# Entry order, pool data, ring keys and last rows in a one-core macaron decoder block

## The chip, the cores and the metric

The kernel runs on one core of one Trainium2 chip. Five engines work side by side: TensorE (PE, matrix products, with its weight loads as PEld), VectorE (DVE), ScalarE (ACT), GpSimd (POOL) and SyncE (SP, which here only issues transfers). Each engine takes its own instructions strictly in order and waits on semaphores for the others. The metric is the time of one execution on the device in microseconds.

## The reference

Input x is 1024 tokens by 1024 channels in float32. With `rms` a normalisation of each token's row:

```python
h = x + 0.5 * swiglu(rms(x), w1a, w3a, w2a)        # swiglu = (silu(x@w1) * (x@w3)) @ w2, width 2816
u = rms(h)
q, k, v, p, gate_logits = split(u @ W_in)
yA = dilated_mixture_attention(q, k, v) @ W_A      # 3 groups of 4 heads: (window, dilation) (128,1) (512,4) (2048,16)
yB = multiscale_pool(p) @ W_B                      # 4 groups of 128 channels, trailing means over 2, 4, 8, 16
h = h + (sigmoid(gA) * yA + sigmoid(gB) * yB) @ W_o
h = h + 0.5 * swiglu(rms(h), w1b, w3b, w2b)
out = rms(h)
```

## The kernel before, in words

**The products.** Every float32 operand is split in a high part in fp32r (a copy by ACT) and a lower part (the rest, a subtraction by DVE or POOL). A product is then three matmuls: high by high, lower by high, high by lower. The large products go by a seven-product scheme on 2 x 2 blocks. The left operand X (tokens) exists as seven sums: b11, b21, b22 (blocks), t1, t2, t3, t4 (sums of blocks). Class `Quad` holds the four blocks of one right operand (weights); `operand(m)` makes the m-th sum of weights (for m6 two sums on DVE, L345 and L347, for m7 one, L351) and splits it (`split`: ACT L303, then POOL or DVE L306); `run(m)` puts 12 matmuls of 128x512 on PE (L314). m1 uses b11, m2 b21, m3 b22, m4 t4, m5 t1, m6 t2, m7 t3, in the order 1, 6, 2, 7, 5, 4, 3.

**The entries.** At three places the X sums of a new left operand must first be made: at the start of the first FFN (f1, from the start to about 70 us), at the combined input projection (mix, from about 667) and at the second FFN (f2, from about 1297). There `Entry.run` interleaves the making of the sums with products m1 and m2, which need only b11 and b21. Token tiles 4 to 7 come one after the other. For tile t: the row is scaled by its norm (`scaled_rows`, DVE L267, with the difference for t3 by POOL L430), transposed on PE (L381 and L455), copied by ACT (L382 in `Rows`, L398 in `Parts`) and its lower parts are made by DVE (L385 in `Rows`, L401 in `Parts`); the sums t1 (L460), t2 (`second`, L441) and t4 (`fourth`, L445) are made by DVE in between. Each tile takes two products, i before its transposes and k behind them, two operands for products to come, and `out(i)` and `out(k)`, which carry results out of PSUM (DVE or ACT). `more(0)` is the operand for product m6, the first one behind the entry, and `more(1)` the one after. All of this is an order written out by hand under a manual schedule, so the order of the calls is the order in each engine's queue.

**The pairs.** In `up` a `Pair` joins two quads (gate and up projection of the FFN). When it is done, `Pair.parts` makes the sums of its result for the second product (L582, L587, L588, L592) and spills each to DRAM through SP (L577).

**From mix to attention.** The input projection's products are spread over 'items'. At fixed places before the end loads for the attention stage are put on SP: the four pool blocks of 1 MiB (`load_pool`, L1234), which lie in places of X sums no longer needed (groups 2 and 3 in b11, groups 0 and 1 in b21), the values (`load_values`, L1227) and the weights and gates of the first branch product (`load_branch`, L1238 and L1239). `late_w` (L1184) and the gates (L1061) are stored through SP in the same stretch. Then attention runs: scores `s` (L1545), transposes `tp` (L1592), `o` (L1625), and the branch product `yp` (L1679), which takes its left operand from the pool blocks and its right from `wab`. The keys and queries of a head group are loaded by `load_ring` (L1197, L1198) into a ring of eight places.

**The output projection.** `step_o(i)` multiplies by part i of W_o (L1918). Its operand is split by `hi_o` (ACT L1901) and `lo_o` (DVE L1905). The last steps stand between the transposes for f2 (`rows_first2`, whose `lower` and `keep` are L385 and L389).

**The last product.** `Down` multiplies by w2 in steps (L753), splits its operands (L711, L715), sums weights where needed (L731) and adds into the rows (L758). At the last but one product, `low_half` squares the lower half of a row (ACT L2083), adds the epsilon (DVE L2084) and multiplies the half by the final gain (DVE L2085); at the last one `high_half` (L2090), `power` (L2094, L2095) and `send_out` (L2100 to L2104) finish the row.

Of the kernel before, what the change touches and what calls it, by code (L numbers as in the profile page):

```python
# [10 lines left out]
F32 = mybir.dt.float32  # L11
# [115 lines left out]
def tile_block(  # L127
# [275 lines left out]
    class Entry:  # L403
# [18 lines left out]
        def run(self, high, after, first=0):  # L422
# [11 lines left out]
            for t in range(4, NT):  # L434
# [16 lines left out]
                s = Rows(X, "b22", y[:, HIGHS], t)  # L451
# [4 lines left out]
                r3 = Rows(X, "t3", t3, t)  # L456
                t2 = bank("acc", f"x_t2_{t}")
                if last:
                    r2 = second()
                ve.tensor_tensor(p12, p12, b11, op=OP.subtract)  # L460
                r1 = Parts(X, "t1", p12, t)
                if not last:
                    s.lower()
                self.operand(i + 2)
                self.out(i)
                self.product(k)
                if last:
                    r2.lower()
                    r3.lower()
                    r1.lower()  # L470
                    self.more(1)
                    r4 = fourth()
                    s.lower()
                    r4.lower()
                else:
                    y, t3 = scaled_rows(t + 1)
                    r2 = second()
                    r1.lower()
                    r3.lower()
                    r2.lower()  # L480
                    r4 = fourth()
                    self.operand(k + 2)
                    r4.lower()
                self.out(k)
                after(t)
                if t == NT - 2:
# [3 lines left out]
    class Pair:  # L490
# [80 lines left out]
        def parts(self, place=None):  # L571
# [15 lines left out]
            ve.tensor_tensor(a21, a21, a11, op=OP.subtract)  # L587
            ve.tensor_tensor(a12, a12, a22, op=OP.subtract)  # L588
            spill(6, a12)
            spill(5, a21)  # L590
            e = both[:, lows] if place else self.sv.half_tile("u", f"{j}5")
            ve.tensor_tensor(e, a11, a22, op=OP.add)  # L592
            spill(0, e)

    def up(sv, sums, between, name, room, begun):
# [3 lines left out]
        with tc.manual_schedule():  # L599
# [6 lines left out]
            for k, (q, w, m, out) in enumerate(items):  # L606
# [4 lines left out]
                if k > 0:  # L611
# [4 lines left out]
                    if p is not q:  # L616
                        parts.append(p.parts())
# [224 lines left out]
    def begin_up1():  # L842
# [95 lines left out]
        def after(t):  # L938
            if t + 2 < NT:
                squares(t + 2, square2)  # L940
            if t == 5:
                raws.depth = 8
# [394 lines left out]
    X_mix.update(sums_of_x(mstack.enter_context(sbuf("xb")), "mix", ("b22", "t2", "t3", "t1", "t4")))  # L1337
# [14 lines left out]
    with tc.manual_schedule():  # L1352
# [4 lines left out]
        for k in range(len(items) + 4):  # L1357
# [29 lines left out]
            if k == len(items) - 5:  # L1387
                load_pool(2, "b11", 0)
                load_pool(3, "b11", 1)
            if k == len(items) - 4:  # L1390
                load_values(0, row_part)
                load_branch(0)
            if k == len(items) - 3:
# [822 lines left out]
```

## Time and profile before

| | us |
|---|---|
| three runs | 1952.91, 1947.35, 1949.93; median 1949.93 |
| the profiled execution | 1953.68 |
| its span | 1951.9 |
| PE busy in the span | 1909.9 (98%) |
| DVE, ACT, POOL busy | 1338.1, 777.0, 727.5 |
| moved by DMA | 333.56 MB, 171 GB/s in the mean |

A line of the profile such as `u_mixm<-xhi_t_mix,wc_mixm` names the tile written and the tiles read; f1, mix and f2 are told apart by the names' endings (`u_f1..`, `u_mixm`, `u_f2..`). Times in a timeline are from the span's start. The span counts from the first to the last recorded instruction, so it is a little shorter than the execution's own time.

### The profile page before, as it was taken

The page shows a single profiled execution, that of the slowest core. Times are in us where ns is not written, and L with a number is a line of the kernel's source. Part 1 is how long each engine was busy: PE and PEld are TensorE (multiplying, and loading weights), DVE is VectorE, ACT ScalarE, POOL GpSimd, SP SyncE. Part 2 cuts the span into 40 slices and gives each one's busy share as a digit, 9 for nine tenths or more (in the row PEclk, how much of TensorE's full clock was granted, in tenths as well). Part 3 has the DMA queues.
Part 4 walks back from the last instruction along what each step waited for, and adds up shares of the span by engine and source line. Part 5 has one row for each costly group of instructions (what it writes and reads, how often), then busy time and mean ns, then how long its engine had stood idle before and what let it go on. Part 6 is the DMA issues. An engine that isn't in the chain of part 4 may idle for free. (4 is left out here: it accounts for less than half of the span.)

```text
span 1951.9 us, 24861 instructions
## 1 busy us (share of the span) xinstructions
PE 1909.9 (98%) x8842; PEld 1571.3 (80%) x8842; DVE 1338.1 (69%) x2020; ACT 777.0 (40%) x1396; POOL 727.5 (37%) x555
## 2 busy tenths in 40 slices
PE   9999999999999999999998999999999999999998
PEld 7788888888888877888877888877788888878886
DVE  6777556658676776657874797777666556577777
ACT  6323332333345542334444673263333333333344
POOL 4333333332222344544544265643333333322132
PEclk9999999999999999999999999999999999999999
DMA  4154322336475526764568997642523323454564
GB/s 185 33 197 150 111 87 103 134 114 207 150 240 201 193 81 226 235 228 181 210 249 290 258 248 264 246 172 73 208 92 125 108 86 103 137 195 148 189 215 162
DMA packets 147437, 333.56 MB, mean 171 GB/s; under 512 B 20209, under 2 KB 40945, under 8 KB 145777
## 3 DMA queue, kind: packets, MB, share of 16 engines
q1 hardware_dynamic: 138096, 307.22, 46.8%
q10 hardware_dynamic: 9216, 24.75, 3.6%
q8 instruction: 70, 1.15, 0.2%
q14 instruction: 55, 0.44, 0.1%
HBM read 229.61 MB, written 102.30 MB: 170 GB/s over the span
## 5 line engine op out<-in xcount | busy, mean ns | idle before, releaser
L753 PE MATMUL d_f<-bhi_f,ahi_f 128*128 128x512 f32 x616 | 240.7, 391 | 1.7 <-ACT ahi_f L711 1.2
L753 PE MATMUL d_f<-bhi_f,alo_f 128*128 128x512 f32 x616 | 240.5, 390 | 1.7 <-POOL alo_f L715 1.3
L753 PE MATMUL d_f<-blo_f,ahi_f 128*128 128x512 f32 x616 | 239.7, 389 | 0.0
L715 POOL TENSOR_TENSOR alo_f<-g_f,ahi_f 128x512 fp32r<-128x512 f32 x68 | 96.7, 1439 | 282.9 <-ACT ahi_f L711 282.9
L314 PE MATMUL u_mixm<-xhi_t_mix,wc_mixm 128*128 128x512 f32 x608 | 197.3, 395 | 4.3 <-DVE xlo_t_mix L385 3.2
L314 PE MATMUL u_mixm<-xhi_b_mix,wc_mixm 128*128 128x512 f32 x456 | 149.2, 394 | 3.3 <-DVE y_m L1036 2.0
L314 PEld LDWEIGHTS u_mixm<-xhi_t_mix,wc_mixm 128*128 128x128 f32 x608 | 115.1, 190 | 30.2 <-ACT y_m L1030 3.6
L753 PEld LDWEIGHTS d_f<-bhi_f,alo_f 128*128 128x128 f32 x616 | 115.6, 188 | 28.0 <-POOL alo_f L715 2.6
L753 PEld LDWEIGHTS d_f<-bhi_f,ahi_f 128*128 128x128 f32 x616 | 115.6, 188 | 26.1 <-ACT ahi_f L711 1.6
L753 PEld LDWEIGHTS d_f<-blo_f,ahi_f 128*128 128x128 f32 x616 | 115.7, 188 | 23.8
L314 PE MATMUL u_mixm<-xlo_t_mix,wc_mixm 128*128 128x512 f32 x304 | 119.4, 393 | 0.0
L306 POOL TENSOR_TENSOR wc_mixm<-s_mixm,wc_mixm 128x512 fp32r<-128x512 f32 x52 | 74.2, 1428 | 103.7 <-ACT wc_mixm L303 88.3
L314 PEld LDWEIGHTS u_mixm<-xhi_b_mix,wc_mixm 128*128 128x128 f32 x456 | 85.1, 188 | 24.8 <-POOL wc_mixm L306 3.8
L303 ACT ACTIVATE wc_mixm<-s_mixm 128x512 fp32r<-128x512 f32 x76 | 47.8, 630 | 131.0 <-DVE s_mixm L347 56.7
L314 PE MATMUL u_mixm<-xlo_b_mix,wc_mixm 128*128 128x512 f32 x228 | 88.9, 390 | 0.0
L711 ACT ACTIVATE ahi_f<-g_f 128x1024 fp32r<-128x1024 f32 x84 | 81.8, 974 | 2.6 <-DMA g_f<-gs_f 2.5
L306 POOL TENSOR_TENSOR wc_mixm<-raw,wc_mixm 128x512 fp32r<-128x512 f32 x40 | 57.7, 1444 | 64.8 <-ACT wc_mixm L303 59.2
L1918 PE MATMUL wo<-w_o,o_hi 128*128 128x512 f32 x224 | 69.4, 391 | 0.3 <-ACT o_hi L1901 0.3
L711 ACT ACTIVATE bhi_f<-s_f2w 128x512 fp32r<-128x512 f32 x55 | 32.7, 627 | 91.5 <-DVE s_f2w L731 82.3
L314 PEld LDWEIGHTS u_mixm<-xlo_t_mix,wc_mixm 128*128 128x128 f32 x304 | 57.8, 190 | 12.0
L711 ACT ACTIVATE bhi_f<-s_f1w 128x512 fp32r<-128x512 f32 x55 | 33.1, 630 | 78.5 <-DVE s_f1w L731 73.5
L715 DVE TENSOR_TENSOR alo_f<-g_f,ahi_f 128x1024 fp32r<-128x1024 f32 (+1 forms) x44 | 52.7, 1197 | 7.1 <-ACT ahi_f L711 7.1
(1318 smaller groups left out, 5099.6 us busy)
## 6 DMA issues: line engine op xcount, KB each, us to landing
g_f<-gs_f SPq DMA_DIRECT2D x70, 512.0 KB, 4.5
gs_f<-y_f SPq DMA_DIRECT2D x88, 256.0 KB, 2.2
raw<-in_w2a_dram SPq DMA_DIRECT2D x35, 512.0 KB, 3.9
raw<-in_w2b_dram SPq DMA_DIRECT2D x35, 512.0 KB, 3.9
gs_f<-gb_f SPq DMA_DIRECT2D x46, 256.0 KB, 2.3
raw<-in_w1a_dram SPq DMA_DIRECT2D x22, 512.0 KB, 4.6
raw<-in_w3a_dram SPq DMA_DIRECT2D x22, 512.0 KB, 6.2
raw<-in_w1b_dram SPq DMA_DIRECT2D x22, 512.0 KB, 4.3
```

Of the source, the lines that this page charges most:

```text
L303: ac.activation(w[:, 0], src, AF.Copy)
L306: eng.tensor_tensor(w[:, 1], src, w[:, 0].bitcast(F32), op=OP.subtract)
L314: pe.matmul(p, a, b, start=(start and k == 0 and q == 0), stop=(k == 3 and q == 2), skip_group_check=not start)
L711: ac.activation(hi[:, c], src, AF.Copy)
L715: eng.tensor_tensor(lo[:, d], src[:, o], hi[:, d].bitcast(F32), op=OP.subtract)
L753: pe.matmul(self.banks[m][t], l, r, start=(first and q == 0), stop=(last and q == 2))
L1918: pe.matmul(banks[m][t], l, r, start=(st == 0 and j == 0 and q == 0), stop=(st == 1 and j == 1 and q == 2))
```

## The change

- In `Entry.run`, tiles 4 to 6: the operand for a later product follows its product at once; the lower part of the first sum (t1) comes ahead of the next tile's scaling; `out(k)` comes ahead of the fourth sum. In the last tile the transposes come in the order t3, p12, b22 instead of b22, p12, t3. `more(0)` moves from the end of tile 6 to the end of tile 5. As a count of splits decides which engine makes a lower part, the lower part of f2's m6 is made by POOL instead of DVE.
- In f1 the raw weights are loaded a piece deeper from each tile on.
- In `up`, the three sums of `Pair.parts` are made one per product, in another order, instead of all three behind one product.
- t2 of the mix lies in a pool of its own that lives on into attention. Pool groups 2 and 3 are loaded one product sooner, groups 0 and 1 two products sooner and into t2. The first branch's weights and gates are loaded ahead of the values. The keys of every second use go into quarters of b21's place, and the ring has four places instead of eight.
- In the output projection, the last operand is split behind the first two tiles' lower parts.
- In the last product, the four rows' products with the final gain stand together at the last tile of the last but one product, and the epsilon is added in `power`.

The number of matmuls, of transfers and of ACT instructions stays; DVE has five instructions fewer and POOL one more.

```diff
--- before.py
+++ after.py
@@ -448,42 +448,49 @@
                 self.product(i)
                 if not last:
                     high(t + 1, 0)
-                s = Rows(X, "b22", y[:, HIGHS], t)
+                    self.operand(i + 2)
+                    s = Rows(X, "b22", y[:, HIGHS], t)
+                else:
+                    r3 = Rows(X, "t3", t3, t)
                 p12 = bank("acc", f"x_b12_{t}")
                 for j in range(4):
                     c = slice(j * P, (j + 1) * P)
                     pe.transpose(p12[:, c], y[:, c], ident)
-                r3 = Rows(X, "t3", t3, t)
-                t2 = bank("acc", f"x_t2_{t}")
-                if last:
+                if not last:
+                    ve.tensor_tensor(p12, p12, b11, op=OP.subtract)
+                    r1 = Parts(X, "t1", p12, t)
+                    r3 = Rows(X, "t3", t3, t)
+                    t2 = bank("acc", f"x_t2_{t}")
+                    s.lower()
+                    r1.lower()
+                    self.out(i)
+                    self.product(k)
+                    self.operand(k + 2)
+                    y, t3 = scaled_rows(t + 1)
                     r2 = second()
-                ve.tensor_tensor(p12, p12, b11, op=OP.subtract)
-                r1 = Parts(X, "t1", p12, t)
-                if not last:
-                    s.lower()
-                self.operand(i + 2)
-                self.out(i)
-                self.product(k)
-                if last:
+                    r3.lower()
+                    r2.lower()
+                    self.out(k)
+                    r4 = fourth()
+                    r4.lower()
+                else:
+                    t2 = bank("acc", f"x_t2_{t}")
+                    r2 = second()
+                    ve.tensor_tensor(p12, p12, b11, op=OP.subtract)
+                    r1 = Parts(X, "t1", p12, t)
+                    s = Rows(X, "b22", y[:, HIGHS], t)
                     r2.lower()
                     r3.lower()
+                    self.out(i)
+                    self.product(k)
                     r1.lower()
                     self.more(1)
                     r4 = fourth()
                     s.lower()
                     r4.lower()
-                else:
-                    y, t3 = scaled_rows(t + 1)
-                    r2 = second()
-                    r1.lower()
-                    r3.lower()
-                    r2.lower()
-                    r4 = fourth()
-                    self.operand(k + 2)
-                    r4.lower()
-                self.out(k)
+                    self.out(k)
                 after(t)
-                if t == NT - 2:
+                if t == NT - 3:
                     self.more(0)
 
 
@@ -568,7 +575,7 @@
             for _ in self.parts(place):
                 pass
 
-        def parts(self, place=None):
+        def parts(self, place=None, apart=False):
 
             j, y = self.j, self.y
             lows, highs = slice(0, HALF), slice(HALF, S)
@@ -584,13 +591,13 @@
             spill(1, both[:, highs])
             yield
 
-            ve.tensor_tensor(a21, a21, a11, op=OP.subtract)
-            ve.tensor_tensor(a12, a12, a22, op=OP.subtract)
-            spill(6, a12)
-            spill(5, a21)
             e = both[:, lows] if place else self.sv.half_tile("u", f"{j}5")
-            ve.tensor_tensor(e, a11, a22, op=OP.add)
-            spill(0, e)
+            sums = ((6, a12, a12, a22, OP.subtract), (5, a21, a21, a11, OP.subtract), (0, e, a11, a22, OP.add))
+            for m, to, a, b, how in sums:
+                ve.tensor_tensor(to, a, b, op=how)
+                spill(m, to)
+                if apart:
+                    yield
 
     def up(sv, sums, between, name, room, begun):
 
@@ -614,7 +621,7 @@
                     for g in parts:
                         next(g, None)
                     if p is not q:
-                        parts.append(p.parts())
+                        parts.append(p.parts(apart=True))
             out = items[-1][3]
             out(last, res[-1])
             for g in parts:
@@ -938,8 +945,8 @@
         def after(t):
             if t + 2 < NT:
                 squares(t + 2, square2)
-            if t == 5:
-                raws.depth = 8
+            if t < 6:
+                raws.depth = t + 3
                 raws.load()
 
         entry.run(high, after, 4)
@@ -1334,7 +1341,8 @@
         with tc.manual_schedule():
             down.run(pool, after1, tick)
     dstack.close()
-    X_mix.update(sums_of_x(mstack.enter_context(sbuf("xb")), "mix", ("b22", "t2", "t3", "t1", "t4")))
+    X_mix.update(sums_of_x(xstack.enter_context(sbuf("xt")), "mix", ("t2",)))
+    X_mix.update(sums_of_x(mstack.enter_context(sbuf("xb")), "mix", ("b22", "t3", "t1", "t4")))
 
     def high_mix(t, part):
         if part == 0:
@@ -1384,15 +1392,15 @@
                 nc.sync.dma_start(mask, c_mask)
             if k == len(items) - 12:
                 later.append([k, first_ring()])
-            if k == len(items) - 5:
+            if k == len(items) - 6:
                 load_pool(2, "b11", 0)
                 load_pool(3, "b11", 1)
+            if k == len(items) - 5:
+                load_pool(0, "t2", 0)
+                load_pool(1, "t2", 1)
             if k == len(items) - 4:
+                load_branch(0)
                 load_values(0, row_part)
-                load_branch(0)
-            if k == len(items) - 3:
-                load_pool(0, "b21", 0)
-                load_pool(1, "b21", 1)
         ac.activation(warm, mhalf, AF.Exp)
     assert not later
     mstack.close()
@@ -1461,7 +1469,21 @@
     uses = [hp * GROUPS + g for hp, g, i in slots if i == 0]
 
     def ring_tile(dt, name):
-        return rings.tile([P, S], dt, tag="ring", bufs=8, name=name)
+        return rings.tile([P, S], dt, tag="ring", bufs=4, name=name)
+
+    quarters = [X_mix["b21"][part].rearrange("p k c -> p (k c)")[:, n * S:(n + 1) * S]
+                for n in range(2) for part in range(2)]
+
+    def ring_place(n):
+
+        if n % 2 == 0:
+            return ring_tile
+        places = list(quarters)
+
+        def place(dt, name):
+            t = places.pop(0)
+            return t if dt is F32R else t.bitcast(F32)
+        return place
 
 
     stats = [att_small.tile([P, GROUPS, NT, 4], F32, name=f"stats{hp}") for hp in range(HPAIRS)]
@@ -1775,7 +1797,7 @@
 
     first = first_w_o()
     with tc.manual_schedule():
-        load_ring(uses[1], ring_tile)
+        load_ring(uses[1], ring_place(1))
         load_branch(1)
         factors = [make_factors(hp, eng) for hp, eng in enumerate((gp, ve))]
         combines = [[combine(hp, half, adds, lower) for half in range(2)]
@@ -1802,7 +1824,7 @@
             masked(2 * q + 1)
             u, i = divmod(q, NT // 2)
             if 0 < u < len(uses) - 1 and i == 0:
-                load_ring(uses[u + 1], ring_tile)
+                load_ring(uses[u + 1], ring_place(u + 1))
             if q > 0:
                 advance(splits[q - 1], 2)
             if i > 1 and u + 1 < len(uses):
@@ -1998,13 +2020,11 @@
         lo_o(STEPS - 2)
         inverse(1)
         scaled2(0)
-        hi_o(STEPS - 1)
         inverse(2)
         scaled2(1)
         inverse(3)
         scaled2(2)
         scaled2(3)
-        lo_o(STEPS - 1)
         step_o(STEPS - 4)
         raws.end = len(raws.pieces)
         raws.depth = 4
@@ -2013,6 +2033,7 @@
         step_o(STEPS - 3, range(2))
         lower(0, r[0])
         lower(1, r[1])
+        split_o(STEPS - 1)
         r.append(rows_first2(2))
         step_o(STEPS - 3, range(2, 4))
         lower(2, r[2])
@@ -2081,9 +2102,11 @@
 
         y, st = h_tile(f"n4_{t}"), small.tile([P, 4], F32, tag="nlast", name=f"nst_last{t}")
         ac.activation(y[:, LOWS], h[t][:, LOWS], AF.Square, scale=D ** -0.5, accum_out=st[:, 0:1])
-        ve.tensor_scalar(st[:, 1:2], st[:, 0:1], EPS, None, op0=OP.add)
+        ends[t] = y, st
+
+    def low_rows(t):
+        y, _ = ends[t]
         ve.tensor_tensor(y[:, LOWS], h[t][:, LOWS], final_gain[:, LOWS], op=OP.mult)
-        ends[t] = y, st
 
     def high_half(t):
         y, st = ends[t]
@@ -2091,8 +2114,8 @@
 
     def power(t):
         y, st = ends[t]
-        ve.tensor_tensor(st[:, 2:3], st[:, 2:3], st[:, 1:2], op=OP.add)
-        gp.tensor_tensor(st[:, 3:4], st[:, 2:3], mhalf, op=OP.pow)
+        ve.scalar_tensor_tensor(st[:, 1:2], st[:, 2:3], EPS, st[:, 0:1], op0=OP.add, op1=OP.add)
+        gp.tensor_tensor(st[:, 3:4], st[:, 1:2], mhalf, op=OP.pow)
 
     def send_out(t):
         y, st = ends.pop(t)
@@ -2109,6 +2132,9 @@
             nc.sync.dma_start(out[rows, :], norm_rows(t, final_gain, "n4", own_row))
         elif m == len(DOWN) - 2:
             low_half(4 + t)
+            if t == 3:
+                for u in range(4, NT):
+                    low_rows(u)
         elif m == len(DOWN) - 1:
             high_half(4 + t)
             if t > 0:
```

## The prediction

> **What bounds the kernel now.** I read the page first, then the waits of TensorE, then the granted clock window by window, then the timeline of each long wait.
>
> ```profile
> span 1951.9 us, 24861 instructions
> PE 1909.9 (98%) x8842; PEld 1571.3 (80%) x8842; DVE 1338.1 (69%) x2020; ACT 777.0 (40%) x1396; POOL 727.5 (37%) x555
> ```
>
> The span is 1951.9 us and the profiled execution took 1953.68, so 1.8 us lie around it. The three runs have a median of 1949.93, 3.75 below this execution; I work out differences from the trace and take them off the median. PE is busy 98% of the span, and the change takes no matmul away: it can only shorten waits of PE and stretches in which PE runs at a lower clock. The waits, longest first:
>
> ```profile
> PE u_mixm L314 <- DVE xlo_t_mix L385: 3.2, 1, 3.2
> PE u_f20a L314 <- DVE xlo_t_f L385: 3.2, 1, 3.2
> PE u_f10a L314 <- DVE xlo_t_f L385: 3.1, 1, 3.1
> PE yp L1679 <- DMA wab<-late_w: 2.5, 1, 2.5
> PE yp L1679 <- DMA xhi_b_mix<-pool: 2.3, 1, 2.3
> PE u_f21a L314 <- DVE y_f L529: 1.7, 1, 1.7
> PE x_b L381 <- ACT h_again L389: 1.4, 1, 1.4
> PE d_f L753 <- ACT ahi_f L711: 1.2, 1, 1.2
> ```
>
> The first three are the same place in the three entries: the first matmul after an entry's last product (product m6 of the first quad) waits for the lower part of t3. Two are the start of attention. The last three are one place each: a sum of a pair, the output projection, and the last product. They make 18.6 us. A wait costs more than its length where the clock falls after it (columns: stretch, its length, PE busy and matmuls, granted clock, DMA share, GB/s):
>
> ```profile
> 57.97:61.38 3.41, 1.37 (x6) 1.00 0.00 0
> 61.38:64.80 3.42, 2.31 (x6) 0.50 0.00 0
> 64.80:68.21 3.41, 3.41 (x10) 0.50 0.00 0
> 699.68:703.09 3.41, 1.19 (x6) 1.00 0.00 0
> 703.09:706.50 3.41, 2.45 (x6) 0.50 0.00 0
> 706.50:709.91 3.41, 3.41 (x10) 0.50 0.02 5
> ...
> 1064.90:1068.31 3.41, 0.90 (x7) 1.00 0.98 383
> 1068.31:1071.73 3.42, 2.05 (x6) 0.50 1.02 425
> 1071.73:1075.14 3.41, 2.44 (x14) 0.50 1.01 400
> 1075.14:1078.55 3.41, 3.37 (x14) 0.50 0.69 159
> ...
> 1331.14:1334.55 3.41, 3.41 (x10) 0.50 0.01 2
> 1935.30:1938.71 3.41, 2.11 (x8) 1.00 0.00 0
> ```
>
> The clock changes at edges 3.41 us apart. After a stretch with PE busy 1.37 of 3.41 or less it is halved; after one with 2.11 it is not. It stays halved until a well filled stretch has passed. Half of the busy time at half clock is lost: (2.31+3.41)/2 = 2.9 us after the first entry, (2.45+3.41)/2 = 2.9 in the mix, 3.41/2 = 1.7 in the third entry, (2.05+2.44+3.37)/2 = 3.9 at the start of attention. The Trainium skill ("TensorE: Matmul & The Clock Gate", The HAM clock gate) has such free-running windows of 3413 ns, and puts the clock down after at least one idle window. The trace agrees on the length and not on the rule: windows that were 35 and 40% busy were enough.
>
> **The entries (f1, mix, f2).** The mix, whose last tile begins at 696.2:
>
> ```profile
> 696.40 0.69 DVE L401 TENSOR_TENSOR xlo_t_mix<-x_t,xhi_t_mix 128x512 fp32r<-128x512 f32 x1 [0.66 <-ACT xhi_t_mix L398]
> 697.01 1.79 DVE L345 TENSOR_TENSOR s_mixm<-raw 128x512 f32<-128x512 f32 x1
> 698.84 0.69 DVE L347 TENSOR_TENSOR s_mixm<-s_mixm,raw 128x512 f32<-128x512 f32 x1
> 701.26 0.70 DVE L441 TENSOR_TENSOR x_t<-x_t,h 128x512 f32<-128x512 f32 x1 [1.73 <-ACT xhi_t_mix L382]
> 703.23 0.68 DVE L385 TENSOR_TENSOR xlo_t_mix<-x_t,xhi_t_mix 128x512 fp32r<-128x512 f32 x1
> ...
> 696.97 1.28 POOL L306 TENSOR_TENSOR wc_mixm<-raw,wc_mixm 128x512 fp32r<-128x512 f32 x1 [1.96 <-ACT wc_mixm L303]
> ...
> 700.64 0.59 ACT L382 ACTIVATE xhi_t_mix<-x_t 128x512 fp32r<-128x512 f32 x1
> ...
> 704.05 0.77 PE L314 MATMUL u_mixm<-xhi_t_mix,wc_mixm 128*128 128x512 f32 x1 [3.18 <-DVE xlo_t_mix L385]
> ```
>
> Since the rows come from one timeline per engine, they are to be read together. After tile 6's last lower part (696.40) DVE makes m6's two sums (L345 1.79, L347 0.69). ACT's copy of the result stands ahead of the last tile's copies, so t3's high part is made at 700.64 only; DVE idles 1.73 for it, and from 700.64 to m6 is 3.41 us of second sum, copies and lower parts. The change moves the two sums and their copy to the end of tile 5 and puts t3's transposes first in the last tile. Removed from this chain: 697.01 to 700.64, 3.6 us. Added: DVE reaches the last tile later, by the two sums (2 x 0.69 = 1.4 without a collision) and by handoffs that had another operation to cover them: t1's lower part now stands right behind the copy it needs, and nothing fills the wait for t4's copy (0.66 in the first row stays). I take 0.5 for these in the mix: lag 1.9, m6 earlier by 3.6-1.9 = 1.7. In f1, where also the squares are waited for and the results out are on DVE more often, I take a lag of 2.5 and 1.1 earlier; f2 the same or less.
>
> What is late next: DVE is late by then, so PE stalls earlier, at the second product of tile 6, whose lower operand part and whose row parts come through the engines that made m6's operand. I walk PE's queue with the durations above to a stall of some 3.4 us there, split by two matmuls. PE's idle time before m6 is not gone but moved, and the wait before m6 falls under 1 us. So no halving follows at m6, 2.9 us saved. The moved stall may halve the clock for one window, in which DVE and not PE sets the pace for part of the time: that costs up to 3.41/2 = 1.7, of which about 0.9 reaches m6. In f1 I count it (the window holds 0.8 busy), in the mix half (1.5 busy is between 1.37 and 2.11).
> - f1: 1.1 + 2.9 - 0.9 = 3.1, say 3.0. Bounds: 0 (stall moved, halving moved) and 4.0.
> - mix: 1.7 + 2.9 - 0.4 = 4.2. Bounds 1 and 4.6.
> - f2: 0.9 + 1.7 - 0.4 = 2.2. Bounds 0 and 3.4 (its walk isn't done row by row; the nearest rows are the mix's).
>
> The raw loads that now go out a tile or two sooner in f1 cost nothing here: they wait only for a free place, and DMA is at 0.00 in the first windows above. In f2 POOL instead of DVE makes m6's lower part; POOL's 1.28 has a whole tile to hide in.
>
> **Start of attention.** PE's first branch product needs wab, then four pool blocks of 1 MiB (columns of the queue: issue, time on the queue):
>
> ```profile
> 1047.63 0.34 SPq L1234 DMA_DIRECT2D xhi_b_mix<-pool  x1
> 1055.57 1.41 SPq L1227 DMA_DIRECT2D v_in<-v  x2
> 1057.02 0.89 SPq L1238 DMA_DIRECT2D wab<-late_w  x1
> 1058.64 0.43 SPq L1234 DMA_DIRECT2D xhi_b_mix<-pool  x1
> ...
> DMA to landing us min/median/max: 10.8/10.8/10.8
> ```
>
> wab is issued at 1057.02 and lands 10.8 us later, 1067.8: 5.5 MiB after 1047.63 (two pool blocks, 1 MiB each of late_w, gates and v, half for itself) took 20.2 us, 3.7 us a MiB, and the DMA share in the windows of 1064.90 to 1075.14 is 1.0. So it is the amount ahead in the queue that counts, not the time of issue. The change puts the other two pool blocks ahead (2 MiB) and v behind (1 MiB): wab lands 1 MiB later, near 1071.4. Then all pool blocks are there. PE has one wait of about 6 us in place of 2.5, 2.3 and a small one, and half clock until the window edge at 1075.14 rather than 1078.55. PE's work done by 1078.55 was 0.7 + 3.9 = 4.6 us at full clock; after, 1071.4 to 1075.14 gives 1.9, and the other 2.7 are done by 1077.8. Gain 0.7. Bounds: with wab at 1069.5 a filled window ends the half clock one edge sooner, +3; with wab at 1075, -3. The keys that take b21's quarters are behind all this in the queue, are used by the second group only, and b21's last product is long over: nothing.
>
> **Single places.** In the output projection the last split leaves the path of the first lower parts and goes behind them:
>
> ```profile
> 1278.90 1.22 DVE L1905 TENSOR_TENSOR o_lo<-o_sum,o_hi 128x1024 fp32r<-128x1024 f32 x1
> ```
>
> DVE starts L385 1.22 sooner, so the 1.4 wait goes but for 0.2, and the moved split is wanted only by a later step. Take 1.1 of bounds 0 to 1.4. Of a pair's three sums, two leave the queue ahead of L529, each spaced like this one (next start 0.61 later):
>
> ```profile
> 1367.63 0.68 DVE L588 TENSOR_TENSOR y_f<-y_f 128x512 f32<-128x512 f32 x1
> ```
>
> 2 x 0.61 = 1.2 of the 1.7 (bounds 0, if the later sums hold up another sum, to 1.7). They are paid one and two products later, each beside a whole product of PE. In the tail:
>
> ```profile
> 1934.74 0.68 DVE L2085 TENSOR_TENSOR n<-h_last,gain_final 128x512 f32<-128x512 f32 x1
> 1935.34 0.68 DVE L731 TENSOR_TENSOR s_f2w<-raw,raw 128x512 f32<-128x512 f32 x1
> ...
> 1940.16 0.68 DVE L758 SCALAR_TENSOR_TENSOR h_last<-d_f,h_last 128x512 f32<-128x512 f32 x1
> ```
>
> L2085 and the small addition leave the steps, so L731 and with it the operand behind the 1.2 wait come 0.7 sooner a step. But all four row products then stand at the last step ahead of the L758 of 1940.16, 4 x 0.6 = 2.4 us. If the three earlier steps pass on what they save, that L758 is about 1.4 sooner; if only the last does, 0.4 later. Take 1.0.
>
> **Sum:** 3.0+4.2+2.2+0.7+1.1+1.2+1.0 = 13.4. This profile's 1953.7 would become 1940.3; the median 1949.9 - 13.4 = 1936.5.
>
> **Rivals.**
> - *The entries keep a halving each* (0.18): the moved stall is as long as the old one and the clock falls there, with PE the bound in it. Then 1 us an entry: 3+0.7+3.3 = 7.0, 1942.9. For it: the windows at 1.37 and 1.19; against it: two matmuls more in the stall, and DVE as the bound behind it. By the skill's rule in the page named above (only an idle window halves), the split stall would never halve, which would give 13.4+1.7 = 15.1 and 1934.8; the row of 1.37 speaks against it.
> - *Everything at its better end* (0.12): 4.0+4.6+3.4+3+1.4+1.7+1.4 = 19.5, 1930.4. It wants wab early, which the full DMA share speaks against.
> - *The lag eats it, slower* (0.10): DVE's lag at the last tile passes 3.6 us. L345 took 1.79 beside POOL's 696.97 and not 0.69; if both sums and t1's part meet POOL, the lag is 1.9 + 3 x 1.1 = 5.2, m6 is 1.6 late, and there are two stalls and two halvings. Each entry then loses 1.6 + 2.9 = 4.5 for f1 and mix and 1.6 + 1.7 = 3.3 for f2: 12.3 less 3.3 for the single places, 9.0 slower, 1958.9. Against it: POOL is busy 37%. The Trainium skill ("SBUF — State Buffer") says that a DVE operation with two SBUF inputs and a GpSimd operation that reads SBUF lock one another out for a whole instruction; L345's 1.79 is as long as that would make it.
> - *The moved work comes back elsewhere* (0.12): the entries gain 1 each, the wab wait grows by 3 and the tail is 0.4 late: 3-3+2.3-0.4 = 1.9, 1948.0, no measurable change.
>
> **How the numbers follow.** The forecast has 0.48. 0.3%, 5.8 us, is about what a measurement of this kernel can tell from no change: faster is below 1944.1. The forecast, the better end and the halving rival are faster (0.78, less 0.03 for halving with a poor tail); same takes 0.15, slower 0.10. The range goes from the better end with half the spread of the three runs (2.6), 1928, to 1949, which takes in the fourth rival and leaves the slower one out.
>
> **What would show it.** Right: at f1, mix and f2 the wait for L385 falls below 1 us, the window after m6 has clock 1.00, and a wait for a lower operand part or a bank of 1 to 3 us appears one and a half products earlier; one wait at wab of 5 to 7 us and none for pool; the L529 wait at 0.5; the wait for h_again at 0.2; none for ahi_f at the end. Wrong: m6 no sooner relative to the entry's first tile, halved windows in both places, or wab later than 1075 against the last mix product.

## The result and the profile after

The changed kernel took 1938.01 us in the median of four runs (1936.67 to 1939.96) beside 1950.08 for the kernel before: a ratio of 0.9939, 95% interval 0.9922 to 0.9956. Five more runs on another occasion gave 1936.18 beside 1948.84, ratio 0.9935, 0.9922 to 0.9949. That is 12.7 us faster, between 9.9 and 15.2 (12.1 in the first four runs). The forecast was 13.4 us and 1936.5.

The profiled execution took 1938.52 us. The first rows of its page:

```profile
span 1936.7 us, 24862 instructions
PE 1900.9 (98%) x8842; PEld 1567.9 (81%) x8842; DVE 1341.3 (69%) x2015; ACT 776.9 (40%) x1396; POOL 730.0 (38%) x556
```

The matmuls are as many as before, and 15.2 us lie between the two spans. The longest waits of PE after the change:

```profile
PE yp L1701 <- DMA wab<-late_w: 3.3, 1, 3.3
PE u_f12a L314 <- ACT y_f L527: 3.3, 1, 3.3
PE u_mixm L314 <- ACT y_m L1032: 2.8, 1, 2.8
PE u_f21a L314 <- ACT y_f L527: 2.3, 1, 2.3
...
PE u_f21a L314 <- DVE y_f L536: 0.5, 1, 0.5
...
PE x_b L381 <- ACT h_again L389: 0.3, 1, 0.3
```

The waits on L385 before m6, 9.5 us in sum, have left the list. Three waits on ACT (L527 and L1032 are copies of results, `out(i)`) stand in their place, 8.4 us in sum and nearly as long. The two waits at the start of attention have become one. L529 (now L536) went from 1.7 to 0.5, h_again from 1.4 to 0.3, ahi_f from 1.2 to none. So little of the long waits was saved in the entries. The windows, and what they say of the clock:

```profile
48.75:52.16 3.41, 1.14 (x6) 1.00 0.01 2
52.16:55.58 3.42, 2.43 (x6) 0.50 0.00 0
55.58:58.99 3.41, 3.41 (x11) 0.50 0.45 154
...
687.04:690.46 3.42, 1.52 (x7) 1.00 0.01 2
1059.10:1062.51 3.41, 0.31 (x2) 1.00 1.02 368
1062.51:1065.92 3.41, 3.41 (x10) 0.50 1.02 418
1308.27:1311.68 3.41, 1.16 (x5) 1.00 0.01 2
1311.68:1315.10 3.42, 3.42 (x9) 0.50 0.35 143
```

In f1 and f2 the moved stall halves the clock (1.14 and 1.16 of 3.41 busy ahead of it). In the mix it doesn't (1.52 busy). At the start of attention one window is halved, not three. Half of the busy time at half clock is now (2.43+3.41)/2 + 3.41/2 + 3.42/2 = 6.3 us, beside 2.9+2.9+3.9+1.7 = 11.4 before, 5.1 less. That is what PE lost, and not all of it is time: a halved window costs nothing where PE would only have waited, as the traces show below.

Where the time went can be read by setting each matmul's start against the same matmul's start before. The lead of the changed kernel at some places, in us; the last two columns are two kernels described below in which the stage is unchanged:

| stage (time before) | lead at its start | at its end | gained | gained by e2 or e3, stage unchanged |
|---|---|---|---|---|
| f1 (25 to 76) | 0.36 | 2.02 | 1.7 | e2 1.0, e3 1.0 |
| f1's pairs (76 to 150) | 2.02 | 2.98 | 1.0 | e2 0.0 |
| mix entry (673 to 712) | 2.83 | 6.57 | 3.7 | e2 0.1, e3 1.2 |
| start of attention (1063 to 1090) | 6.42 | 10.37 | 4.0 | e3 1.6 |
| attention, output projection (1090 to 1300) | 10.37 | 10.40 | 0.0 | e2 0.3 |
| f2 (1300 to 1337) | 10.40 | 12.69 | 2.3 | e2 1.6, e3 0.0 |
| L529 (1369 to 1375) | 12.69 | 13.89 | 1.2 | e2 0.0 |
| the rest, to the end of the span | 13.89 | 15.15 | 1.3 | |

The last column is a warning: a stage that nobody touched differed by 1 to 1.6 us from one execution to the next. In the entries the clock did it. The profiled execution before was the slowest of its runs (1952.91 to 1947.35 without the profile): its clock was halved for two windows at f1 and the mix, where e3, with the same entries, lost one each. At the start of attention it wasn't the clock: e1 and e3, with that stage unchanged, had three windows halved there as before, but waited 3.7 and 3.4 us for the transfers instead of 4.8. Sums against it come out too high for the median.

### The profile page after: what moved, and what is told of

It is laid out like the page before. It is cut to its first block, busy times and chain, and to the rows that moved or that the text cites. A ratio compares the mean times of both kernels' runs of the same rounds, so it can differ in the third digit from the quotient of the medians.

```text
span 1936.7 us, 24862 instructions
## 1 busy us (share of the span) xinstructions
PE 1900.9 (98%) x8842; PEld 1567.9 (81%) x8842; DVE 1341.3 (69%) x2015; ACT 776.9 (40%) x1396; POOL 730.0 (38%) x556
## 5 line engine op out<-in xcount | busy, mean ns | idle before, releaser
L303 ACT ACTIVATE wc_mixm<-s_mixm 128x512 fp32r<-128x512 f32 x76 | 47.7, 629 | 128.0 <-DVE s_mixm L347 53.5
```

The costliest lines, as they stand in the source:

```text
L303: ac.activation(w[:, 0], src, AF.Copy)
```

## The experiments

**e1 to e3: the parts alone.** Each is the kernel before with one part of the change: the entries (with f1's raw loads), the start of attention, or the three single places.

> The kernel before with the change to the entries alone (Entry.run and the deeper raw loads of f1). Read off the two traces, PE's lead over the kernel before grew by about 1.9 us in f1, 0.8 in f1's pairs behind it, 3.3 in the mix and 1.9 in f2. Theory A (the parts are independent, the entries carry the most): 7 to 8 us faster than before, ratio about 0.996, the waits on L385 at m6 gone, a wait on ACT's result copy of 2 to 3.5 us in its place one product and a half earlier in each entry. Theory B (the gain of the whole came from the start of attention, and the entries only moved their stall): within 2 us of before.

1943.38 beside 1949.21, ratio 0.9971 (0.9959 to 0.9983): 5.7 us faster, 3.3 to 8.0. The waits of PE are those of the whole change: 3.2 us in f1, 2.8 in the mix and 2.2 in f2 for ACT's copies of results. Theory A in direction, with a median below its 7 to 8; theory B's 2 us lies outside the interval.

> The kernel before with the change to the start of attention alone (t2 in a pool of its own, pool blocks sooner, branch ahead of values, ring keys in b21's quarters). Theory A (what the prediction said: the transfers are bound by the amount ahead of wab, 3.3 to 3.7 us a MiB): wab lands 3 us later than before against the last mix product, gain 0.7 us. Theory B (read off the trace after: with more transfers waiting at once a MiB takes less, 3.2 us in the mean and 2.5 in the pool blocks): wab lands only about 1 us later, PE's lead grows by 3 to 4 us up to the first attention slots, and up to 0.9 of it goes again near the fifth head group. Ratio about 0.998 by B, 1.000 by A.

1947.20 beside 1949.21, ratio 0.9993 (0.9983 to 1.0003): 1.4 us faster, from 3.3 faster to 0.6 slower. wab landed 20.9 us after the first pool block was issued. That is 0.7 more than in the profiled execution before, as theory B has it, but 1.9 more than in e1 and e3, which have that stage unchanged (19.0 each): the transfers lie between the two theories. PE's lead grew by 4.0 from 1063 to 1079, of which some 1.5 is not the change, since e1 gained 1.45 and e3 1.6 there without it.

> The kernel before with the three small parts alone: the pair's sums spread, the last split of the output projection behind two lower parts, the four row products of the tail together. Theory A (forecast 1.2 + 1.1 + 1.0 = 3.3 us): ratio about 0.998, PE's wait for L529 near 0.5, for h_again near 0.3, none for ahi_f at the end. Theory B: the output projection gives back part of its 1.1 at a later step, as the trace after says (0.6 stays), and the two pairs of f1 give 0.4 each that was not forecast: about 3.5 us in all.

1946.02 beside 1949.21, ratio 0.9982 (0.9972 to 0.9993): 3.5 us faster, 1.4 to 5.5. Both theories' sizes lie in it. In its trace the wait for L529 is 0.5 and the one before the transposes 0.3, as in the whole change, and there is a new one:

```profile
PE wo L1918 <- ACT h_again L389: 0.3, 1, 0.3
```

This wait of `wo` is what the projection gives back: the lead there goes from 4.54 to 5.07, so 0.5 of 1.1 stays. f1's pairs gave 1.0 (from 1.55 to 2.58). The three ratios multiply to 0.9946; the whole change is at 0.9935 (0.9922 to 0.9949), so the parts add up as far as these runs can tell.

**e4: m6's operand back at the end of tile 6.**

```diff
-                if t == NT - 3:
+                if t == NT - 2:
                     self.more(0)
```

> The changed kernel with m6's operand back at the end of tile 6, all else kept. Theory A (the gain at m6 comes from m6's operand leaving the chain of the last tile): the wait before m6 is back at 2 us or more with half clock behind it, the stall at tile 7's first product is gone or under 1 us, and the entries lose most of their gain: 4 to 7 us slower than the changed kernel. Theory B (it comes from the transposes' order in the last tile and the earlier sums): within 2 us of the changed kernel.

1938.79 beside 1949.21, ratio 0.9944 (0.9929 to 0.9959): not told apart from the changed kernel. Theory A falls. The wait before m6 did come back, at 1.9 to 2.0, and the stall before tile 7's product shrank, in f1 to 1.5. The mix's row:

```profile
PE u_mixm L314 <- DVE xlo_t_mix L385: 1.9, 1, 1.9
```

So the place of m6's operand decides where PE waits; what that is worth is read across the traces below. ACT shows why its early place brought a stall; the mix of the changed kernel, then of e4 in its last tile:

```profile
688.19 0.63 ACT L303 ACTIVATE wc_mixm<-s_mixm 128x512 fp32r<-128x512 f32 x1 [2.14 <-DVE nst L263]
...
690.68 0.61 ACT L1032 ACTIVATE y_m<-u_mixm 128x512 f32<-128x512 f32 x1
```

```profile
694.69 0.63 ACT L303 ACTIVATE wc_mixm<-s_mixm 128x512 fp32r<-128x512 f32 x1 [2.14 <-DVE s_mixm L347]
695.23 0.58 ACT L382 ACTIVATE xhi_t_mix<-x_t 128x512 fp32r<-128x512 f32 x1
```

In both, ACT sits idle 2.14 us in front of m6's copy until DVE has made the sums. In the changed kernel the tile's three copies and the result copy L1032 are queued behind it, and the next product, tile 7's first, waits for the bank that L1032 has yet to read: PE starts it at 691.34, when L1032 ends. In e4 the last tile's copies stand behind it.

**e5: m6's operand in the middle of tile 6**, behind the tile's second product.

```diff
                     self.operand(k + 2)
+                    if t == NT - 2:
+                        self.more(0)
                     y, t3 = scaled_rows(t + 1)
...
-                if t == NT - 3:
-                    self.more(0)
```

> The changed kernel with m6's operand in the middle of tile 6, behind the tile's second product, instead of at the end of tile 5. In the trace after, ACT waits 2.14 us for m6's sums in the mix with the tile's copies and the result copy L1032 queued behind it, and PE stalls 2.78 us for L1032. Theory A (the moved stall is ACT's order, not DVE's amount of work): that stall falls under 1 us in all three entries, no halved clock in front of m6 in f1 and f2, m6 0 to 1 us sooner, 1 to 4 us faster than the changed kernel. Theory B (DVE's amount of work sets m6, the stall only moves again): the stall comes back as long before tile 7's transposes, within 1 us of the changed kernel.

1940.77 beside 1951.91, ratio 0.9940 (0.9920 to 0.9959): theory B. The stall at L1032 is short now, and one as long stands before tile 7's transposes, here in the mix (2.8 in f1, 2.3 in f2):

```profile
PE x_t L381 <- POOL s_mixt L430: 2.7, 1, 2.7
```

With the operand in three places (e4, e5, the change) the time is the same within the runs. Theory A's other signs failed too: the clock is halved ahead of m6 in f1 and f2.

**e11: what of the entries gains.** e4 with the last tile in the order of before (b22, t1, t3 transposed in turn; the lower parts behind the product). Only tiles 4 to 6 are changed.

> e4 with the last tile's own order of before (b22, t1, t3 transposes; lower parts of t2, t3, t1 behind the product). Left of the change to the entries is only what it does to tiles 4 to 6. e4 showed that the place of m6's operand isn't what gains. Theory A (the order of the last tile gains, since t3's copy no longer stands behind m6's copy and b22's): the wait before m6 goes from 1.9 back to about 3.2 us, with a halved window in each entry, 3 to 6 us slower than e4. Theory B (the earlier operands and sums of tiles 4 to 6 gain): the wait grows by under 0.5 us, within 1.5 us of e4.

1942.16 beside 1950.62, ratio 0.9953 (0.9935 to 0.9971). The wait before m6 nearly doubles against e4, to 3.7 or 3.8 us in all three entries, with halved windows behind all three,

```profile
PE u_mixm L314 <- DVE xlo_t_mix L385: 3.7, 1, 3.7
```

and ACT makes t3's copy third, not second, behind m6's:

```profile
696.00 0.63 ACT L303 ACTIVATE wc_mixm<-s_mixm 128x512 fp32r<-128x512 f32 x1 [2.14 <-DVE s_mixm L347]
...
697.01 0.59 ACT L382 ACTIVATE xhi_t_mix<-x_t 128x512 fp32r<-128x512 f32 x1
```

That is theory A's sign, but a longer wait is not yet a loss. In the mix m6 starts only 0.5 us later than in e4, which is the copy; the other 1.3 of the longer wait is PE arriving sooner. The 3.4 us between the two medians are in the expected range, but the intervals of the two ratios overlap, so the size is not settled.

**Read across the traces: where m6 starts.** A wait can grow because its end moves or because PE arrives sooner, so here m6's start itself is taken, from the entry's first product on, and then the time of the 60 matmuls from m6 on. In brackets stands how many windows of each stretch were halved.

| | f1: to m6 | then 60 | mix: to m6 | then 60 | f2: to m6 | then 60 |
|---|---|---|---|---|---|---|
| before | 48.1 | 16.4 (2) | 33.4 | 16.5 (2) | 33.8 | 15.3 (1) |
| e2, entries as before | 48.1 | 15.3 (1) | 33.5 | 16.4 (2) | 33.8 | 13.8 |
| e7, entries as before | 48.1 | 15.3 (1) | 33.4 | 13.8 | 33.8 | 15.3 (1) |
| the change | 48.8 (2) | 14.1 | 32.6 | 13.6 | 33.2 (1) | 13.6 |
| e12, the change again | 48.1 (1) | 13.7 | 32.6 | 13.6 | 33.2 | 13.6 |
| e1, the change's entries | 48.1 (1) | 13.7 | 32.6 (1) | 13.6 | 33.2 (1) | 13.6 |
| e4 | 47.8 | 14.1 | 31.6 | 15.3 (1) | 32.4 | 15.3 (1) |
| e11 | 48.3 | 15.3 (1) | 32.1 | 15.3 (1) | 32.7 | 16.4 (2) |

Four things can be read from it. Behind m6 a halved window costs 1.5 us and two cost 2.6, and in the kernel before it varies by execution how many there are. Ahead of m6, in the changed kernel, one halved window costs nothing in the mix and in f2: the mix from its first product to m6 in e1 and then in e12,

```profile
667.37:699.93 32.56, 29.46 (x145) 0.95 0.14 49
666.43:699.04 32.61, 28.27 (x146) 1.00 0.14 49
```

takes as long with a halved window as without. PE is busy 1.2 us longer in e1 and idle that much less. Behind the stall e12 has two more waits of PE in the mix,

```profile
PE x_t L381 <- POOL s_mixt L430: 0.9, 1, 0.9
PE x_b L381 <- DVE xlo_t_mix L401: 0.6, 1, 0.6
```

of which e1 has only 0.3 for xlo_t_mix left: the slower matmuls fill them. Third, with m6's operand at its old place (e4) m6 starts 0.3 to 0.9 us sooner than in the change, but it has a wait in front of it, and in two entries of three the clock fell behind that wait. Fourth, against before, the new order of tiles 4 to 6 (e11) brings m6 1.3 and 1.0 us sooner in the mix and f2 and not at all in f1, and the last tile's order (e4 beside e11) 0.4 to 0.5 in each. So what the early operand buys is a stall in a place where half clock costs nothing; it does not bring m6 sooner. Over the three entries e4 is 0.7 us slower than the change and 1.8 slower than e12, not the 4 to 7 of e4's theory A.

**e8 and e9: the clock by itself.** e8 is the kernel before with twelve matmuls more behind each entry's last product, into the same bank, so the second term is added twice there.

```diff
+                w_k = self.todo[k][0].w.get(self.todo[k][1]) if last else None
                 self.product(k)
                 if last:
+                    self.sv.product(self.banks[k], w_k, "b21", start=False)
```

> The kernel before with twelve more matmuls (2.7 us at full clock) behind the last product of each entry, which fill the wait before m6; they add the second term once more, so the results of the last quad's two columns are not the reference's. Nothing else is moved. Theory A (half of each entry's loss is the clock): m6 starts at the same time as before, the clock stays 1.00 behind it in all three entries, and 2.9 + 2.9 + 1.7 = 7.5 us are gained by added work. Theory B (the records of the clock don't cost what they say): no gain, or a loss up to 3 x 2.7 if the filling runs into m6.

1945.89 beside 1951.91, ratio 0.9970 (0.9957 to 0.9983): 5.9 us faster, 3.3 to 8.4, by work added. The 6.8 us from m6 on, in e8 and then in e3, whose entries are those of before (columns as in the windows above):

```profile
61.60:68.40 6.80, 6.44 (x28) 1.00 0.00 0
700.90:707.70 6.80, 6.57 (x29) 1.00 0.03 9
1321.70:1328.50 6.80, 6.55 (x29) 1.00 0.09 19
```

```profile
61.80:68.60 6.80, 6.63 (x22) 0.75 0.00 0
701.40:708.20 6.80, 6.62 (x22) 0.75 0.02 5
1325.50:1332.30 6.80, 6.58 (x22) 0.75 0.08 21
```

PE starts 28 or 29 matmuls in that time instead of 22: 6 or 7 by 0.23 us, about 1.5 us an entry, three times. m6 itself starts as before (48.1, 33.5 and 33.8 us after the entry's first product). Theory A; its 7.5 lies in the interval, and 3 x 1.5 too.

e9 is e4 with six matmuls into a bank that nobody reads, behind the last product of each entry. e10 adds nine ahead of the first branch product, in the wait for wab.

```diff
                     self.product(k)
+                    idle, hi = bank("mm", f"idle_{self.sv.name}"), X["b21"][0]
+                    for _ in range(6):
+                        pe.matmul(idle, hi[:, 0, :P], hi[:, 0, :], start=True, stop=True)
...
+        for _ in range(9 if n == 0 else 0):
+            pe.matmul(p, y_pool[2][:, 0, :P], y_pool[2][:, 0, :HALF], start=True, stop=True)
```

> The kernel of e4 (the change with m6's operand at the end of tile 6) with six matmuls (1.4 us at full clock) into a bank that nobody reads, behind the last product of each entry, in a wait of 1.9 to 2.0 us. All results are the reference's. Theory A (a halved clock behind m6 costs what its record says: one window, 1.7 us, in the mix and in f2 of e4): clock 1.00 behind all three m6, the wait down to some 0.5 us, m6 at the same time, 2 to 4 us faster than e4 and than the change. Theory B (added matmuls only take time, since m6 follows DVE and the clock matters little): within 1 us of e4.

> e9 with nine more matmuls (2.0 us) ahead of the first branch product, in the 3.3 us wait for wab. Theory A: the window of that wait is over half filled, so the half clock behind it (one or two windows) goes: 1.7 to 3.4 us faster than e9, the first yp no later. Theory B: the halving comes from the stretch as a whole, or the wait varies with the transfers, and the filling gains nothing or costs up to 1 us.

e9: 1937.59 beside 1950.62, ratio 0.9933 (0.9917 to 0.9950). e10: 1937.88, ratio 0.9930 (0.9915 to 0.9945). In both the clock is 1.00 for 6.8 us behind all three m6. In e10 the filling did not do what it was for:

```profile
1057.45:1060.87 3.42, 1.53 (x7) 1.00 1.03 402
1060.87:1064.28 3.41, 3.41 (x10) 0.50 1.03 420
```

A window with 1.53 busy halved the clock, one with 1.52 in the changed kernel's mix did not. But the edge does not lie there, as rows of e1 and then of e12 show:

```profile
1056.11:1059.52 3.41, 1.99 (x16) 1.00 1.02 389
1059.52:1062.94 3.42, 1.19 (x4) 0.50 1.00 416
```

```profile
1306.23:1309.64 3.41, 1.58 (x7) 1.00 0.01 2
1309.64:1313.05 3.41, 2.98 (x12) 1.00 0.06 23
```

Here 1.99 halved it and 1.58 did not. Beside the change at 0.9935, neither kernel is shown to be faster, so in time both theories of e9 and e10 stay open. In e9's trace theory A's price of the clock holds: from the first product to 60 matmuls behind m6 the mix takes 45.4 us and f2 46.1, beside 47.0 and 47.7 in e4 and 46.2 and 46.8 in the change. But PE's wait for wab was 5.3 us in that execution, 1.9 more than in e4, which took back a part.

**e6 and e7: the order of the loads.** e6 is the changed kernel with the values ahead of the first branch's weights and gates, e7 the kernel before with only these two exchanged.

> The changed kernel with the values' loads (1 MiB) ahead of the first branch's weights and gates again. Theory A (the DMA queue is full and in order, a MiB ahead costs 2.5 to 3.7 us): wab lands 2.5 to 3.7 us later against the last mix product, PE's wait for it goes from 3.3 to 6 or 7 us, half clock one window longer. Theory B (transfers share the engines, the order matters little): wab's wait within 1 us of 3.3.

> The kernel before with only the first branch's weights and gates put ahead of the values. Theory A (amount ahead): wab lands about 2.5 to 3.5 us sooner and PE's 2.5 us wait for wab nearly goes, but the pool blocks of groups 0 and 1 still stand behind and land as before: the wait for pool grows to 4 to 5 us, total lead within 1 us of before. Theory B (wab alone holds PE): 2 us or more faster at the first attention slots.

e6 took 1942.82 and e7 1949.44, one execution each. First rows of their waits, e6 and e7 in turn:

```profile
PE yp L1701 <- DMA wab<-late_w: 9.0, 1, 9.0
```

```profile
PE yp L1679 <- DMA xhi_b_mix<-pool: 4.7, 1, 4.7
```

e6 has 5.7 us more of wait than the change for 1 MiB ahead (4.7 more than e12), beyond theory A's 3.7. The queue says why, with the longest of SP's own waits below:

```profile
1047.26 7.13 SPq L1234 DMA_DIRECT2D v_in<-v  x2
1055.31 0.61 SPq L1245 DMA_DIRECT2D wab<-late_w  x1
```

```profile
SPq L1234 <- DMA xlo_t_mix<-pool: 6.5, 1, 6.5
```

The second half of the values was issued only when the last pool block had landed, though it is written to another tile (why it waits for that one is not shown), and wab, which in the changed kernel is issued at 1048.61, stood behind it until 1055.31. e7 is theory A: the wait moves from wab to the pool blocks.

**e12: the change once more.**

> The changed kernel itself, in more runs, to narrow its interval (0.9922 to 0.9956). Theory A (the forecast's 13.4 us, ratio 0.9931, holds in the median): interval around 0.993. Theory B (the three parts timed alone, 0.9971, 0.9993 and 0.9982, multiply to 0.9946, since the halved windows of the profiled execution before were more than the usual): 0.9945 or so, 10 to 11 us. The filled kernels stood at 0.9933 and 0.9930: by A they are no faster than the change, by B some 2 us faster.

Its figures are those at the top. The median is nearer theory A, but the interval, 0.9922 to 0.9949, takes in B's 0.9945 too.

## Why the prediction was right, and where its steps were not

**The whole.** 13.4 forecast, 12.7 measured (9.9 to 15.2). The direction, the size and the order of the parts held; single steps did not. That the sum came so near is in part luck: the parts timed alone make 10.5 (0.9946), with the entries 3.7 short of their term.

**The entries (9.4 forecast, 5.7 alone, 3.3 to 8.0).** The kind of gain was right: in none of the four traces of the changed entries (the change, e1, e6, e12) is a window behind m6 halved, the stall moved as foreseen, and the prediction's own sentence that the idle time before m6 "is not gone but moved" holds. Three sizes were off.

- *m6 sooner.* Forecast 1.1, 1.7 and 0.9 in f1, mix and f2; 0, 0.8 and 0.6 by the table. The step that failed is the chain: it held that m6's operand in front of the last tile's copies costs 3.6 us, and that taking it out brings m6 sooner. e4 puts it back, and m6 starts sooner still. What brings it sooner is the order of tiles 4 to 6 and, with 0.4 to 0.5, that of the last tile. The deeper loads of raw weights in f1 were not tried by themselves; f1's m6 came no sooner with them.
- *The halvings behind m6.* They were priced by the windows of one execution, 2.9 us at f1 and the mix. How many windows a wait halves differs from one execution to the next, none to two in the table: in e3, with the entries of before, it was one each (1.7).
- *The halving of the moved stall.* Forecast at 0.9, 0.4 and 0.4; one window cost nothing in the mix and f2, and in f1 a second one cost 0.7. The remark that DVE and not PE sets the pace there was right (in the mix PE has two more waits to come, for POOL and DVE), and truer than its price.

With m6 1.4 sooner in sum and one window of 1.6 saved in each entry this makes 6.2, near the 5.7 measured.

The moved stall was taken for a wait at tile 6's second product, for operand parts; it stood at tile 7's first, for ACT's result copy queued behind m6's copy (the list of signs had "or a bank"). The length, "some 3.4 us", was right for f1 (3.3) and too long for the mix (2.8) and f2 (2.3).

**The start of attention (0.7 forecast, 1.4 alone, -0.6 to 3.3).** The single wait came, with 3.3 to 5.3 us in seven executions and not 6. The step that was off is the 3.7 us a MiB. These windows run from the first pool block's issue to wab's landing, before and then after:

```profile
1047.63:1067.82 20.19, 17.55 (x84) 1.00 0.97 330
```

```profile
1041.20:1062.06 20.86, 17.56 (x84) 1.00 0.96 353
```

One MiB more took 0.7 us more: the rate rose from 330 to 353 GB/s, though the engines had been counted as full. Of the 330, the first 9.4 us had 310 with a DMA share of 0.89. Other executions put the difference higher: this stretch took 18.8 to 20.2 us in four with the old order of loads (before, e1, e3, e8) and 20.9 to 22.9 with the new. So amount ahead orders the landings (e6, e7), but a MiB cost less than 3.7 when more was issued early, and it cost more where SP's issue had itself to wait for a landing (e6). What gains is the clock: over this stage PE is idle 3.5 to 5.0 us with the old order and 3.4 to 5.4 with the new, but before, e1 and e3 have three windows halved behind the two waits (e8 one), while the change, e2, e4, e11 and e12 have one behind the single wait (e5 and e9 two).

**The single places (3.3 forecast, 3.5 alone, 1.4 to 5.5).** L529 1.2 as forecast. The projection 0.5 and not 1.1: a product two steps on waits for h_again (0.3 in the list). That the total fits is luck in part: f1's pairs made up for the projection. The tail is as forecast: the wait for ahi_f is gone, and the four row products stand where they were expected,

```profile
1922.61 2.49 DVE L2109 TENSOR_TENSOR n<-h_last,gain_final 128x512 f32<-128x512 f32 x4
1925.01 0.68 DVE L765 SCALAR_TENSOR_TENSOR h_last<-d_f,h_last 128x512 f32<-128x512 f32 x1
```

with the addition behind them at 1925.01, 15.15 us before its old time of 1940.16 in an execution that led by 14.0 when the tail began: 1.1 gained, 1.0 forecast. But the forecast's 1.0 doesn't follow from the figures beside it (four steps of 0.7 less 2.4 give 0.4). In the trace PE's lead grows by 1.9 from 1933 to 1940, as the wait goes, and 0.8 of it is lost again at the four products. f1's pairs, which spread their sums too, gave about 1.0 that the prediction did not count; two waits of 0.3 on L303 in the kernel before went with them.

**The rivals.** The lag did not eat the gain: DVE's two sums took 0.68 and 0.69 in the new place, with no collision. The halving rival's condition came true in two entries of three (in all three in e1, in one in e12), but not its price, as it had PE for the bound behind the stall. Half the spread of the three runs, used for the range, is 2.8 and not 2.6, which leaves its end at 1928. "Everything at its better end" and "comes back elsewhere" did not happen.

## What to carry to other kernels

An engine's in-order queue that waits for another engine holds up everything behind it; moving the waiting instruction moves the stall, and only less work on the chain, or a wait where it is cheap, brings time. Here the stall is cheap where a later wait for another engine takes up what half clock adds. Judge an order by when the next product starts, not by how long PE waits for it. Price a clock loss from several executions, since the same wait may halve no window, one or two. For transfers, put first what is needed first, look at what each issue waits for, and expect that early issue may raise the rate as well.

## What the runs showed of the hardware

In the fourteen traces every window of 3.41 us at full clock with PE busy 1.5 us or less was followed by half clock (the first microseconds of the span aside), and none with more than 2.0. In between both happened (1.53 in e10 and 1.99 in e1 halved it, 1.52 in the change and 1.58 in e12 did not), so busy time as the profile gives it does not place the edge, and what does stays open. At half clock, windows busy up to 2.45 us kept it, one with 2.80 (e11) released it and one with 3.27 (e1) did not. Where the edges fall changes from execution to execution, and with it how many windows are halved; that alone moved unchanged entries by 1 to 1.6 us; runs of the kernel before spread from 1945.94 to 1956.70. Twelve added matmuls in each of three waits made the kernel before 5.9 us faster (3.3 to 8.4). A halved window in the mix cost 1.5 us behind m6 (13.8 us for 60 matmuls in e7, 15.3 in e3) and nothing ahead of it (32.6 us up to m6 in e1 and e12).
